# Turning six of eight token tiles with VectorE block transposes and SBUF transfers instead of TensorE transposes

## The chip, the cores and the metric

The kernel runs on one core of one Trainium2 chip. The metric is the device time of one execution in microseconds (us), lower is better. The core has five engines that run their own instruction streams and wait for each other through semaphores: TensorE (PE, matmuls), VectorE (DVE), ScalarE (ACT), GpSimd (POOL) and SyncE (SP), which here issues nearly all DMA transfers on one queue.

## The reference, cut to what matters

One layer of a hybrid decoder over 1024 tokens of width 1024, all in float32. Two branches (a Conformer convolution and a sliding-window attention) are merged into `mixed`; then

```python
h = layer_norm(DEEPNORM_ALPHA * h + mixed @ w_out, ln1_g, ln1_b)
up = causal_dwconv(h @ ffn_w_up, ffn_dw, ffn_dw_b)
u, g = jnp.split(up, 2, axis=-1)
f = (jax.nn.gelu(g, approximate=False) * u) @ ffn_w_down
return layer_norm(DEEPNORM_ALPHA * h + f, ln2_g, ln2_b)
```

The change concerns the step between the first `layer_norm` and `h @ ffn_w_up`. The layer norm works on rows of tokens (a token per partition, 1024 channels along the free dimension); the product with `ffn_w_up` needs `h` with channels on the partitions. Between the two, every tile of 128 tokens must be turned from 128 tokens x 1024 channels into 8 blocks of 128 channels x 128 tokens.

## The kernel before

Every float32 product is made of three matmuls of rounded parts: an operand is split into a high part (cast by ACT) and a low part (subtraction on DVE, or on POOL). The FFN products follow a Strassen-like scheme, in which sums of quadrants of `h` (called B11, B21, BT1 to BT4 and B22) are formed by DVE, split, and multiplied with sums of quadrants of the weights.

**The w_out stage.** The loop at line 1477 goes over the token tiles in the order 3, 7, 2, (the two leftover meta rows, -1), 6, 0, 4, 1, 5. `out_rows(i)` loads the tile's residual rows from DRAM (`h0d`) into one of two row buffers in `OB` (`RT`), multiplies in two halves of 512 channels (24 matmuls each, into PSUM tiles `ps_w` of which there are three), adds each half to the rows on DVE (L1339), collects the statistics (L1340, L261, ACT's L268 and three short DVE steps), normalises in place (L1361) and stores the rows to `h1d`. A row buffer is loaded anew when its rows have been stored and turned.

**The turn.** `turn(i, ...)` lets PE transpose the eight 128x128 blocks (L1375) into `ps_h`, and ACT evacuates each with the norm's gain and bias as per-partition scalars (L1385) into `h1F`, the place of the turned tile in `FA`. A tile is turned while the next tile is multiplied: its eight transposes stand between the two halves of the next tile (for tile 3 after the second half of tile 7), put there with `behind`. Tile 5, the last, is turned inside the first products of the FFN.

**The order of DVE.** For tiles 0, 4, 1 and 5 the DVE instructions are chained with `line(ins)`: each must come after the one before in program order, whether or not a later one would be ready. Chained are the adds, statistics and norms of these tiles (`pin = line`), and the work on the FFN's operands that lies between them: `w_first` (splits of up-projection weights, L1406 and sums L1423), `split_of(sub, q)` (cast on ACT at L1276, subtraction on DVE at L1281), and `form_t2`, `form_t3`, `form_t4` (sums of quadrants, L1285). `sub` 1 is the part of the tokens in tiles 2, 3, 6, 7, `sub` 0 that in tiles 0, 1, 4, 5, of which `EARLY` columns belong to tiles 0 and 4 and `LATE` ones to 1 and 5. What stands between a tile's halves is written in this table:

```python
work = {0: [(w_first, 2), (split_of, 1, B11), (split_of, 1, B21), (split_of, 1, B22)],
        4: [(w_first, 3), (split_of, 1, BT2), (w_first, 3), (form_t4, 1)],
        1: [(form_t3, 1), (split_of, 0, B11, EARLY), (form_t2, 0, EARLY), (w_first, 5)],
        5: [(w_first, 6)]}
```

`quadrant(sub, kk, h)` is half the channels (`kk`) of one pair of tiles: for `sub` 1, B11 and B21 come from tiles 2 and 3, B22 from tiles 6 and 7; for `sub` 0 and early columns, B11 comes from tile 0, and `form_t2` subtracts quadrants of tile 0 from those of tile 4 (first half of the channels, then second). After tile 4 come the splits of BT4 and BT1 of `sub` 1 and `edges` (two boundary columns, L1469).

DMA instructions are issued by SP (`load`) in the order that the scheduler gives them; only DVE's chain and PE's turns are ordered by hand here.

Of the kernel before, what the change touches and what calls it, by code (L numbers as in the profile page):

```python
# [25 lines left out]
AF = mybir.ActivationFunctionType  # L26
# [3 lines left out]
P = 128  # L30
D = 1024
KC = D // P
# [29 lines left out]
SUB = [(0, 258), (258, HW)]  # L62


RK_TURN, RK_SPLIT, RK_EVAC, RK_START, RK_QKV, RK_RESID, RK_ATT = 450, 500, 600, 1000, 10000, 20000, 30000
# [59 lines left out]
def tile_hybrid_layer(  # L125
# [3 lines left out]
    nc = tc.nc  # L129
# [5 lines left out]
    def load(o, i):  # L135
        return nc.sync.dma_start(out=o, in_=i)
# [5 lines left out]
    def f32(ap):  # L142
        return ap.bitcast(F)

    def after(ins, first):

        tc.add_manual_dep(ins.ins, first.ins.name, mybir.DependencyInfo(
            mybir.DependencyClass.NoSync, mybir.DependencyReason.SCHED_ONLY), reason="order of work")

    @contextmanager  # L150
    def rank(p):

        saved = tc.cur_priority
        tc.cur_priority = p
        yield
        tc.cur_priority = saved
# [10 lines left out]
    RHC = arena.tile([P, 8384], R, name="RHC")  # L167
    RHO = arena.tile([P, 8384], R, name="RHO")
    OB = arena.tile([P, 4 * U], F, name="OB")
# [6 lines left out]
    h0d = dpool.tile([U, D], F, name="h0d")  # L176
    h1d = dpool.tile([S, D], F, name="h1d")
# [39 lines left out]
    cols = const.tile([P, N_COLS], F, name="cols")  # L217
# [13 lines left out]
    g1col = lambda k: colA[:, 58 + k:59 + k]  # L231
    b1col = lambda k: colA[:, 66 + k:67 + k]
# [450 lines left out]
    bias, bias0 = (bias_t[:, a:b].rearrange("p (u h c) -> p u h c", u=2, h=NH // 2)  # L683
                   for a, b in ((0, NH * KW), (NH * KW, N_BIAS)))
# [60 lines left out]
    src = ps[:16, :P].rearrange("p (g d) -> p g d", d=HD)  # L745
    nc.scalar.copy(VA[:16, 0, :, 0], src)
    nc.vector.tensor_tensor(VA[:16, 0, :, 1], src, f32(VA[:16, 0, :, 0]), OP.subtract)
    for q4 in range(2):
# [4 lines left out]
        src = ps[:, :].rearrange("p (n g d) -> p n g d", g=2, d=HD)  # L753
# [31 lines left out]
    ahead = chunks_done[first_chunk + 2 * KC + 7]  # L785
# [6 lines left out]
    for h in range(NH):  # L792
        g, r = divmod(h, 4)
        o = ps[:2, h * 16:(h + 1) * 16]
# [34 lines left out]
    for g in range(NKV):  # L829
# [3 lines left out]
        src = ps[:16].rearrange("p (r q) -> p r q", r=4)[:, :, 0:2]  # L833
# [3 lines left out]
    for g in range(NKV):  # L837
        o = po[:, g * 8:g * 8 + 8]
# [21 lines left out]
    for i in range(NB):  # L860
        for g in range(NKV):
            q = load_q(g, i) if i else q0[g]
# [6 lines left out]
            for u in range(2):  # L869
# [3 lines left out]
                for h in range(2):  # L873
                    o = ps[:, h * KW:h * KW + w]
# [8 lines left out]
                if not i:  # L883
                    f = first[u]
                    src = ps[:, :2 * KW].rearrange("p (h c) -> p h c", h=2)
# [9 lines left out]
            for h in range(2):  # L895
                for u in range(2):
                    j = h * 2 + u
# [68 lines left out]
    OC = late.tile([P, 8320], R, name="OC")  # L966
# [124 lines left out]
    RT = OB[:, 0:2048]  # L1091
# [131 lines left out]
    def h1F(sub, h, k):  # L1223
        o = h1_at(sub, h * KC + k)
        return FA[:, o:h1_at(sub, h * KC + k + 1)]
# [28 lines left out]
    def line(ins):  # L1254

        if lined:
            after(ins, lined[-1])
        lined.append(ins)
        return ins
# [46 lines left out]
    def split_of(sub, q, cs=slice(None)):  # L1306
        b11, b12, b21, b22 = blocks(sub)
        src = {B11: b11, B21: b21, BT2: T2_AT[:, :b22.shape[1]], BT4: b21, BT1: b11, BT3: b12, B22: b22}[q]
        bsplit(sub, q, src, cs)
# [1 line left out]

    WO_ORDER = (4, 5, 0, 1, 2, 3, 6, 7)
    edge = const.tile([P, KC, 2], F, name="edge")
    r_next = [1]

    def out_rows(i, between=(), work=()):


        n, u = (P, 2 + i * P) if i >= 0 else (2, 0)
        if n == P:  # L1320
            o = r_next[0] % 2 * 1024
            r_next[0] += 1
            whole = RT[:, o:o + 1024]
            load(whole, h0d[u:u + n, :])
        else:
            whole = OB[:, 3072:4096]
        r = whole[:n]
        order = WO_ORDER if i != 5 else (0, 1, 2, 3, 6, 7, 4, 5)
        turned = None
        st = small.tile([P, 2, 6], F, name="st")  # L1330
        pin = line if i in (0, 4, 1, 5) else lambda ins: ins
        for half in range(2):
            hs = slice(half * 512, half * 512 + 512)
            ps = pat.tile([P, 512], F, name="ps_w", tag="mm", bufs=3)
            if n == P:
                last = product(ps, [(mixed(i, k, 0), mixed(i, k, 1), wo[k][0][:, hs], wo[k][1][:, hs])
                                    for k in order], turned)
                with rank(RK_TURN):
                    pin(nc.vector.tensor_tensor(r[:, hs], ps, r[:, hs], OP.add))  # L1339
                    pin(nc.vector.bn_stats(st[:, half], r[:, hs]))  # L1340
                turned = None
                if between[half:] and between[half]:
                    turned = turn(*between[half], behind=[last])
                if half == 0:
                    for f, *x in work:
                        f(*x)
                continue

            for j in range(4):
                nc.tensor.matmul(ps[:2], sel[:, j // 2 * 2:j // 2 * 2 + 2], two_parts[j // 2][j % 2][:, hs],  # L1350
                                 start=j == 0, stop=j == 3)
            nc.scalar.copy(r[:, hs], ps[:2])
        if n < P:
            q = FA[:2, 0:1024]
            load(q, h0d[0:2, :])
            nc.vector.tensor_tensor(r, r, q, OP.add)
        with rank(RK_TURN):
            (mu, rs), = ln_stats([(r, n)], half_stats=st if n == P else None)
            for a in (512, 0) if i == 5 else (None,):
                x = r if a is None else r[:, a:a + 512]  # L1360
                ins = pin(nc.vector.tensor_scalar(x, x, mu, rs, OP.subtract, OP.mult))  # L1361
        if n == P:
            load(h1d[u - 2:u - 2 + P, :], r)
        else:
            load(ed, r)
            for t in range(2):
                load(edge[:, :, t], dram(ed, t * D, [[1, P], [P, KC]]))
        return whole, n, ins

    def turn(i, r, n, ins, banks=None, behind=None, upper=False):  # L1370
        with rank(RK_TURN):
            for j, k0 in enumerate((4, 0) if upper else (0, 4)):
                ps = banks[j] if banks else pat.tile([P, 512], F, name="ps_h", tag="s", bufs=2)
                for k in range(4):
                    ins = nc.tensor.transpose(ps[:, k * P:(k + 1) * P], r[:, (k0 + k) * P:(k0 + k + 1) * P], ident)  # L1375
                    if behind:
                        after(ins, behind[-1])
                        behind.append(ins)
                for k in range(k0, k0 + 4):
                    src = ps[:, (k - k0) * P:(k - k0 + 1) * P]  # L1380
                    h, jj = divmod(i, 4)
                    sub = 0 if jj < 2 else 1
                    a = 2 + jj * P - SUB[sub][0]
                    dst = h1F(sub, h, k)[:, a:a + P]
                    nc.scalar.activation(dst, src, AF.Identity, bias=b1col(k), scale=g1col(k))  # L1385
        return behind[-1] if behind else None


    RING = [RHO[:, i * 1024:(i + 1) * 1024] for i in range(4)]
    RING += [None] * 4  # L1390
# [73 lines left out]
    def edges():  # L1464
        with rank(RK_TURN):
            first, second = (FA[:, h * 2064:h * 2064 + 2064].rearrange("p (k n) -> p k n", n=258)[:, :, 0:2]
                             for h in range(2))
            for t, c, op in ((edge, 58, OP.mult), (first, 66, OP.add)):
                line(nc.vector.tensor_tensor(first, t, colA[:, c:c + KC].unsqueeze(2).to_broadcast([P, KC, 2]), op))  # L1469
            nc.vector.memset(second, 0.0)  # L1470

    ahead = []
# [4 lines left out]
    for i in (3, 7, 2, -1, 6, 0, 4, 1, 5):  # L1477
        if i == -1:
            out_rows(i)
            continue  # L1480
        rows = out_rows(i, ahead, work.get(i, ()))
        ahead = [None, (i, *rows)] if i == 3 else [(i, *rows)]
        if i == 3:
            two_rows(7, rows[2])
        if i == 7:
            for a, (hi, lo) in zip(two_sum, two_parts):
                after(split(a, hi, lo, True), rows[2])
            two_stack.close()
            W2.append(wo_stack.enter_context(tc.tile_pool(name="w2", bufs=1, side="right", reuse_waits="tile")).tile(
                [P, 2048], R, name="W2"))  # L1490
        if i == 0:
            form_t2(1)
        if i == 4:
            split_of(1, BT4)
            split_of(1, BT1)
            edges()
        if i == 1:
            split_of(1, BT3)
            split_of(0, B21, EARLY)
            form_t3(0, EARLY)  # L1500
            form_t4(0, EARLY)
# [64 lines left out]
    for c in range(FC):  # L1566
# [8 lines left out]
        for subs in passes:  # L1575
            last = subs == passes[-1]
            w_next = iter(range(7))
            a, b = SUB[subs[0]][0], SUB[subs[-1]][1]
            i = max(a, 2)
# [189 lines left out]
    rows, stats = {}, {}  # L1769
# [159 lines left out]
```

## Time and profile before

| what | value |
|---|---|
| median of 3 runs | 1234.69 us (1234.56 to 1234.72) |
| profiled execution | 1234.65 us, span 1232.9 us, granted clock 0.998 |
| PE, DVE, ACT busy, share of the span | 99%, 88%, 47% |
| w_out stage on PE | 489.58 us (first `ps_w` matmul) to 587.66 us (first FFN matmul) |
| `ps_h` transposes in the stage | 56, 272 ns each by themselves, pipelined |
| DMA in the whole kernel | 210.62 MB, mean 171 GB/s |

All times are positions in one profiled execution, counted from the start of its span. In a row of a timeline the first number is the start, the second the duration (both us), then come the engine, the line of the kernel, the operation, output<-input and, in square brackets, how long the engine had been idle before and what it was waiting for. In the chain of waits a row gives start, duration, engine, output and line. PE's matmuls overlap, so the chain's durations (which add up) are used for PE.

### The profile page before, as it was taken

The page shows a single profiled execution, that of the slowest core. Times are in us where ns is not written, and L with a number is a line of the kernel's source. Part 1 is how long each engine was busy: PE and PEld are TensorE (multiplying, and loading weights), DVE is VectorE, ACT ScalarE, POOL GpSimd, SP SyncE. Part 2 cuts the span into 40 slices and gives each one's busy share as a digit, 9 for nine tenths or more (in the row PEclk, how much of TensorE's full clock was granted, in tenths as well). Part 3 has the DMA queues.
Part 4 walks back from the last instruction along what each step waited for, and adds up shares of the span by engine and source line. Part 5 has one row for each costly group of instructions (what it writes and reads, how often), then busy time and mean ns, then how long its engine had stood idle before and what let it go on. Part 6 is the DMA issues. An engine that isn't in the chain of part 4 may idle for free.

```text
span 1232.9 us, 21777 instructions
## 1 busy us (share of the span) xinstructions
PE 1223.6 (99%) x8564; PEld 1141.3 (93%) x8564; DVE 1084.5 (88%) x1840; ACT 584.4 (47%) x1065; POOL 15.0 (1%) x19
## 2 busy tenths in 40 slices
PE   9999999999999999999999999999999999999997
PEld 8999999999999999888999999999999998888886
DVE  8899989999879798659899999998999986995697
ACT  7532346654265233435655545555455553544331
POOL 1000000000000010000000000000000000000000
PEclk9999999999999999999999999999999999999999
DMA  7284834412255544322255555554465568997722
GB/s 280 74 277 101 213 96 112 129 55 73 85 153 175 180 140 136 116 73 87 69 182 197 193 191 197 191 187 137 167 210 190 182 230 305 395 334 295 255 87 86
DMA packets 104726, 210.62 MB, mean 171 GB/s; under 512 B 28520, under 2 KB 42394, under 8 KB 104624
## 3 DMA queue, kind: packets, MB, share of 16 engines
q1 hardware_dynamic: 88624, 198.16, 48.6%
q10 hardware_dynamic: 16000, 11.07, 2.9%
q8 instruction: 67, 1.10, 0.4%
q14 instruction: 35, 0.29, 0.1%
HBM read 147.59 MB, written 60.38 MB: 169 GB/s over the span
## 4 chain that ended last, share of the span: by engine, by line
PE 98%; DVE 1%; ACT 0%; issue 0%; DMA 0%; POOL 0%; DVEq 0%; POOLq 0%
PE px L1596 14%; PE py L1596 9%; PE ps_x L1742 9%; PE ps_z L330 8%; PE ps_z L329 8%; PE ps_z L325 8%; PE ps_z L1742 8%; PE pw L1596 5%; PE pz L1596 5%; PE ps_p L325 2%; PE ps_p L329 2%; PE ps_p L330 2%; PE ps_w L329 2%; PE ps_w L330 2%; PE ps_w L325 2%; PE ps_z L565 2%
## 5 line engine op out<-in xcount | busy, mean ns | idle before, releaser
L715 DVE SCALAR_TENSOR_TENSOR FA<-cin,cols,FA 128x1026 f32<-128x1026 f32 x120 | 152.3, 1278 | 0.9
L330 PE MATMUL ps_z<-RHO,wlo 128*128 128x256 f32 (+2 forms) x324 | 103.6, 320 | 0.0
L329 PE MATMUL ps_z<-RHO,whi 128*128 128x256 f32 (+2 forms) x324 | 103.5, 319 | 0.0
L330 PE MATMUL ps_z<-RHC,wlo 128*128 128x256 f32 (+2 forms) x324 | 103.4, 319 | 0.0
L329 PE MATMUL ps_z<-RHC,whi 128*128 128x256 f32 (+2 forms) x324 | 103.4, 319 | 0.0
L325 PE MATMUL ps_z<-RHC,whi 128*128 128x256 f32 (+2 forms) x324 | 103.2, 319 | 0.0
L325 PE MATMUL ps_z<-RHO,whi 128*128 128x256 f32 (+2 forms) x324 | 103.2, 318 | 0.0
L294 ACT CAST whi<-wr 128x1024 fp32r<-128x1024 f32 x37 | 38.9, 1051 | 107.4 <-PE ps_z L329 85.1
L1405 ACT CAST RHO<-wr 128x512 fp32r<-128x512 f32 x92 | 55.3, 619 | 26.2 <-DMA wr<-in_w_up_dram 12.2
L1406 DVE TENSOR_TENSOR RHO<-wr,RHO 128x512 fp32r<-128x512 f32 x92 | 62.4, 690 | 5.2 <-ACT RHO L1405 4.9
L325 PEld LDWEIGHTS ps_z<-RHO,whi 128*128 128x128 f32 x324 | 60.9, 188 | 4.5
L329 PEld LDWEIGHTS ps_z<-RHO,whi 128*128 128x128 f32 x324 | 60.9, 188 | 4.2
L325 PEld LDWEIGHTS ps_z<-RHC,whi 128*128 128x128 f32 x324 | 60.9, 188 | 4.1
L329 PEld LDWEIGHTS ps_z<-RHC,whi 128*128 128x128 f32 x324 | 61.0, 188 | 4.1
L330 PEld LDWEIGHTS ps_z<-RHO,wlo 128*128 128x128 f32 x324 | 61.0, 188 | 4.0
L330 PEld LDWEIGHTS ps_z<-RHC,wlo 128*128 128x128 f32 x324 | 61.0, 188 | 3.9
L1423 DVE TENSOR_TENSOR wr<-wr 128x512 f32<-128x512 f32 x88 | 60.9, 692 | 0.2
L297 DVE TENSOR_TENSOR wlo<-wr,whi 128x1024 fp32r<-128x1024 f32 x35 | 42.7, 1221 | 12.0 <-ACT whi L294 11.6
L1608 ACT COPY FA<-px 128x514 f32<-128x514 f32 (+2 forms) x23 | 13.1, 569 | 71.1 <-PE px L1596 71.0
L1405 ACT CAST ws<-wr 128x512 fp32r<-128x512 f32 x60 | 36.1, 618 | 20.9 <-DVE wr L1423 11.8
L722 ACT ACTIVATE FA<-ps_z,cols 128x258 f32<-128x258 f32 (+2 forms) x48 | 26.1, 543 | 39.4 <-PE ps_z L330 39.0
L1406 DVE TENSOR_TENSOR ws<-wr,ws 128x512 fp32r<-128x512 f32 x60 | 40.6, 688 | 3.6 <-ACT ws L1405 3.5
(487 smaller groups left out, 3492.2 us busy)
## 6 DMA issues: line engine op xcount, KB each, us to landing
wr<-in_w_up_dram SPq DMA_DIRECT2D x44, 512.0 KB
wr<-in_w_z_dram SPq DMA_DIRECT2D x30, 512.0 KB
fd<-FA SPq DMA_DIRECT2D x44, 256.0 KB
OB<-in_w_down_dram SPq DMA_DIRECT2D x19, 512.0 KB
qt<-qd SPq DMA_DIRECT2D x28, 256.0 KB
td<-OB SPq DMA_DIRECT2D x12, 512.0 KB
sums<-fd SPq DMA_DIRECT2D x12, 512.0 KB
sd<-sums SPq DMA_DIRECT2D x12, 512.0 KB
```

Source lines behind the costliest of these rows:

```text
L294: ins = nc.scalar.copy(hi, raw)
L297: return (nc.vector if quick else nc.gpsimd).tensor_tensor(lo, raw, f32(hi), OP.subtract)
L325: ins = nc.tensor.matmul(ps, ah, bh, start=i == 0, stop=False)
L329: nc.tensor.matmul(ps, ah, bl, start=False, stop=False)
L330: last = nc.tensor.matmul(ps, al, bh, start=False, stop=i == n - 1)
L715: nc.vector.scalar_tensor_tensor(acc[c], cin[:, j:j + U], wc, acc[c], OP.mult, OP.add)
L722: nc.scalar.activation(t, ps, AF.Tanh, bias=bcol(14 + i), scale=0.5)
L1405: nc.scalar.copy(hi, src)
L1406: ins = nc.vector.tensor_tensor(lo, src, f32(hi), OP.subtract)
L1423: ins = nc.vector.tensor_tensor(*x)
L1596: ins = nc.tensor.matmul(o, x[:, ks], bmat(sub, q, hl, k), start=first and k + j == 0, stop=k == 3 and j == 2, skip_group_check=not first)
L1742: nc.tensor.matmul(bank[:, cs], l[:, ts], r[:, ws], start=first and a and x + k == 0, stop=z and x == len(ops) - 1 and k == 2, skip_group_ ...
```

## The change

Six tiles (3, 7, 2, 6, 0, 4) are no longer turned by PE. For each of them `turn_dma` lets DVE transpose the 32x32 blocks of the normalised rows (one instruction of 128x1024) into a buffer in `OB` (one place for tiles 3, 7, 2, 6, another for 0, 4), and then moves the blocks between partition groups with 16 transfers from SBUF to SBUF, each of 32 partitions by 256 words, into a place in `OC` or `RHC`. ACT's eight evacuations per tile read that place instead of PSUM. Tiles 1 and 5 are turned by PE as before.

The stores of the rows, the transfers and the row loads of all tiles are chained in a written order (`in_turn`): store of tile i, its 16 transfers, the row load of the tile after next, and so on. In DVE's written order the transposes of tiles 0 and 4 are entries of their own (`line`): tile 0's behind its norm, tile 4's behind the splits of BT4 and BT1 and ahead of `edges`. Those of tiles 3, 7, 2 and 6 come after their norm and are not in the chain. The table `work` is unchanged.

```diff
+    NROW = (3, 7, 2, 6, 0, 4, 1, 5)
+    NEXT_ROWS = dict(zip(NROW, NROW[2:]))
+    moves, fetched = [], {}
+
+    def in_turn(ins):
+        if moves:
+            after(ins, moves[-1])
+        moves.append(ins)
+
+    def fetch(i):
+        o = (NROW.index(i) + 1) % 2 * 1024
+        fetched[i] = RT[:, o:o + 1024]
+        in_turn(load(fetched[i], h0d[2 + i * P:2 + (i + 1) * P, :]))
...
-            o = r_next[0] % 2 * 1024
-            r_next[0] += 1
-            whole = RT[:, o:o + 1024]
-            load(whole, h0d[u:u + n, :])
+            if i not in fetched:
+                fetch(i)
+            if not moves[1:]:
+                fetch(NROW[1])
+            whole = fetched[i]
...
                 if between[half:] and between[half]:
                     turned = turn(*between[half], behind=[last])
+                    if between[half][0] in NEXT_ROWS:
+                        fetch(NEXT_ROWS[between[half][0]])
...
-            load(h1d[u - 2:u - 2 + P, :], r)
+            in_turn(load(h1d[u - 2:u - 2 + P, :], r))
...
+    TURN_AT = {3: (OC, 4144, 2048), 7: (OC, 5168, 2048), 2: (OC, 6192, 2048), 6: (OC, 7216, 2048), 0: (RHC, 2096, 3072), 4: (RHC, 3120, 3072)}
+
+    def turn_dma(i, r, norm):
+        t, o, b = TURN_AT[i]
+        blocks, cols = OB[:, b:b + 1024], f32(t[:, o:o + 1024])
+        with rank(RK_TURN):
+            ins = nc.vector.transpose(blocks.rearrange("p (q k j) -> p q k j", q=4, k=KC),
+                                      r.rearrange("p (k q j) -> p q k j", k=KC, q=4))
+            after(ins, norm)
+            if i in (0, 4):
+                line(ins)
+            for a in range(4):
+                for q in range(4):
+                    in_turn(load(cols[32 * q:32 * q + 32, a * 256:(a + 1) * 256],
+                                 blocks[32 * a:32 * a + 32, q * 256:(q + 1) * 256]))
+            if i in NEXT_ROWS:
+                fetch(NEXT_ROWS[i])
...
+            src = cols.rearrange("p (a k j) -> p k a j", a=4, k=KC)
+            for k in range(KC):
+                nc.scalar.activation(h1F(sub, h, k)[:, a:a + P].rearrange("p (a j) -> p a j", a=4), src[:, k],
+                                     AF.Identity, bias=b1col(k), scale=g1col(k))
...
         rows = out_rows(i, ahead, work.get(i, ()))
-        ahead = [None, (i, *rows)] if i == 3 else [(i, *rows)]
+        ahead = [] if i in TURN_AT else [(i, *rows)]
+        if i in TURN_AT and i != 4:
+            turn_dma(i, rows[0], rows[2])
...
         if i == 4:
             split_of(1, BT4)
             split_of(1, BT1)
+            turn_dma(i, rows[0], rows[2])
             edges()
```

More of the change, by code (lines that the diff above doesn't have):

```diff
@@ L1313, in tile_hybrid_layer @@
     edge = const.tile([P, KC, 2], F, name="edge")
-    r_next = [1]
+    NROW = (3, 7, 2, 6, 0, 4, 1, 5)
[9 more added lines that the diff above has]
+        in_turn(load(fetched[i], h0d[2 + i * P:2 + (i + 1) * P, :]))
     def out_rows(i, between=(), work=()):
@@ L1386, in turn @@
         return behind[-1] if behind else None
+    TURN_AT = {3: (OC, 4144, 2048), 7: (OC, 5168, 2048), 2: (OC, 6192, 2048), 6: (OC, 7216, 2048), 0: (RHC, 2096, 3072), 4: (RHC, 3120, 3072)}
[14 more added lines that the diff above has]
+                fetch(NEXT_ROWS[i])
+            h, jj = divmod(i, 4)
+            sub = 0 if jj < 2 else 1
+            a = 2 + jj * P - SUB[sub][0]
+            src = cols.rearrange("p (a k j) -> p k a j", a=4, k=KC)
+            for k in range(KC):
+                nc.scalar.activation(h1F(sub, h, k)[:, a:a + P].rearrange("p (a j) -> p a j", a=4), src[:, k],
+                                     AF.Identity, bias=b1col(k), scale=g1col(k))
     RING = [RHO[:, i * 1024:(i + 1) * 1024] for i in range(4)]
```

## The prediction

> **What bounds the kernel now.** I read the page first, then the chain of work that ended last around the changed stage, then each engine's timeline between 488 and 606 us, and last the DMA issues of SP.
>
> ```profile
> PE 1223.6 (99%) x8564; PEld 1141.3 (93%) x8564; DVE 1084.5 (88%) x1840; ACT 584.4 (47%) x1065; POOL 15.0 (1%) x19
> ```
>
> TensorE (PE) is busy for 99% of the span, so whatever is taken off it is worth time, as long as nothing else becomes late. The chain, from the turn of tile 1 on:
>
> ```profile
> 581.50 0.87 PE ps_h L1375 x8
> ...
> 587.83 1.41 PE px L1596 x12
> ...
> 602.65 1.15 DVE OA L1281
> 603.85 1.58 PE pw L1596 x11
> ```
>
> Eight PE transposes of one tile cost 0.87 us of the chain. The w_out stage ends at 587.83, where the first product of the FFN starts. At 603.85 the chain passes from VectorE (DVE) to PE: there DVE is already level with PE. How full DVE is inside the stage (columns: PE, PEld, DVE, ACT, POOL busy, clock, DMA share, GB/s):
>
> ```profile
> 544.20:585.70 41.50, 41.50 (x201) 34.71 (x200) 36.87 (x59) 21.57 (x48) 0.00 (x0) 1.00 0.24 90
> ```
>
> DVE works 36.87 of 41.50 us, in an order written out by hand, so it stands still whenever the head of that order is not ready. These are the entries on which the change acts:
>
> ```profile
> 540.73 0.69 DVE L1339 TENSOR_TENSOR OB<-ps_w,OB 128x512 f32<-128x512 f32 x1 [4.91 <-PE ps_w L330]
> ...
> 543.34 0.81 DVE L1361 TENSOR_SCALAR OB<-OB,mv,sd 128x1024 f32<-128x1024 f32 x1
> ...
> 546.18 0.69 DVE L1339 TENSOR_TENSOR OB<-ps_w,OB 128x512 f32<-128x512 f32 x1 [2.03 <-PE ps_w L330]
> ...
> 550.98 1.22 DVE L1281 TENSOR_TENSOR RHC<-FA,RHC 128x1024 fp32r<-128x1024 f32 x1
> 552.53 0.69 DVE L1339 TENSOR_TENSOR OB<-ps_w,OB 128x512 f32<-128x512 f32 x1 [0.32 <-PE ps_w L330]
> ...
> 571.18 0.17 DVE L1469 TENSOR_TENSOR FA<-edge,cols 128x16 f32<-128x16 f32 x1
> ...
> 574.87 0.70 DVE L1285 TENSOR_TENSOR FA<-FA 128x520 f32<-128x520 f32 x1
> 575.60 0.70 DVE L1285 TENSOR_TENSOR OB<-FA 128x520 f32<-128x520 f32 x1
> ...
> 579.43 0.81 DVE L1361 TENSOR_SCALAR OB<-OB,mv,sd 128x1024 f32<-128x1024 f32 x1
> ...
> 587.87 0.69 DVE L1339 TENSOR_TENSOR OB<-ps_w,OB 128x512 f32<-128x512 f32 x1 [2.14 <-PE ps_w L330]
> ```
>
> In order: tile 6's second half is added, after 4.91 us of waiting for PE; its norm ends (543.34+0.81 = 544.15); tile 0's first half is added; the split of B22 (sub 1), which needs tiles 6 and 7; tile 0's second half; the edges, right behind the splits after tile 4's norm; the two subtractions of form_t2 (sub 0, early columns), which need tile 4; tile 1's norm, end 580.24; the last half of tile 5.
>
> **The change, part by part.**
>
> *Removed.* 6 tiles x 0.87 us = 5.2 us of PE. Three of the six (tiles 3, 7, 2) lie ahead of tile 0, so tile 0 begins 2.6 us earlier.
>
> *Added on DVE.* Per tile one block transpose of 128x1024 f32; the trace has none. Bounds: 0.81 (L1361) and 2.44, twice the 1.22 of L1281; both rows have the same shape. I take 1.2, the duration of L1281, nearest in shape (it too rewrites 128x1024 words into another buffer; L1361 works in place). Nothing below zero is possible for an added instruction. Tile 6's falls into the 2.03 us in which DVE waited at 546.18 and is hidden there, though its consumers see it; those of tiles 0 and 4 stand in the written order and cost 1.2 each.
>
> *Added on SP.* Per tile 16 transfers of 32 partitions by 1 KB, all on SP's one queue behind the tile's store, and the next row load behind them. The SP rows:
>
> ```profile
> 534.53 0.24 SPq L136 DMA_DIRECT2D ed<-OB  x1
> ...
> 569.02 0.32 SPq L136 DMA_DIRECT2D h1d<-OB  x1
> 571.69 0.32 SPq L136 DMA_DIRECT2D OB<-h0d  x1
> ...
> 1160.90 0.47 SPq L136 DMA_DIRECT2D FA<-fd  x1
> 1161.41 0.47 SPq L136 DMA_DIRECT2D OB<-in_w_down_dram  x1
> ```
>
> The pitch of back-to-back issues is bounded by 0.29 us (0.24 of the smallest, plus the 0.05 by which 0.47 misses the start of the next) and 0.51 (two loads of 512 KB). I take 0.38, nearer the small end, because a transfer has 32 rows. Landing (SP's waits: what it waited for, us in total, times, longest):
>
> ```profile
> SPq L136 <- DMA h1d<-OB: 12.7, 5, 3.1
> ```
>
> The load at 571.69 waited for the store of 569.02, so 512 KB land within 2.67 us of issue. Without the time of the bytes (512 KB at some 390 GB/s, a rate in the rows further down, is 1.3) about 1.4 would be left. I take 1.8. From the transpose's end to the last landing that is 0.1 + 15 x 0.38 + 1.8 = 7.6 us (5.9 to 10.4). The Trainium skill ("DMA: Bandwidth & Descriptors", section "Anatomy of one DMA — SWDGE (gpsimd) path") puts a fixed 2.0 us on a DMA, most of it the write's receipt; as an estimate from it 7.9 instead of 7.6, and 0.6 more in the result below. Its "VectorE: DVE Perf Modes" (section "Rules for kernel authors") speaks against the whole change: a 128x128 transpose belongs on TensorE where a PSUM destination will do, which it did here.
>
> *On ACT* the eight evacuations remain and now read SBUF; I keep their time, and the cast of B22 behind them:
>
> ```profile
> 546.62 2.90 ACT L1385 ACTIVATE FA<-ps_h,cols 128x128 f32<-128x128 f32 x8 [3.90 <-PE ps_h L1375]
> 549.55 1.05 ACT L1276 CAST RHC<-FA 128x1024 fp32r<-128x1024 f32 x1
> ```
>
> *First new wait, B22 behind tile 6.* Norm end 544.15 - 2.6 = 541.55; transpose to 542.75; transfers to 550.35; evacuation to 553.25; cast to 554.3. DVE gets there at 550.98 - 2.6 = 548.4, so it stands for 5.9 us, with tile 0's second half and everything later queued behind. Against before, B22's split is late by 3.3 and the next entry by 3.0 (the 0.32 at 552.53 goes). PE doesn't feel it yet: its three PSUM buffers let it run on.
>
> *Second new wait, form_t2 behind tile 4.* With tile 0's transpose, DVE is 4.2 late; tile 4's transpose runs from 571.18 + 4.2 = 575.4 to 576.6. form_t2 is reached at 574.87 + 5.4 = 580.3, but its first half needs four evacuations of tile 4 (half of 2.90): 576.6 + 7.6 + 1.45 = 585.65. Its second half needs all eight: 587.1, against 575.60 before. DVE is now 11.5 late.
>
> *What this does to PE.* Tile 1 is still turned by PE, between the halves of tile 5, and its norm stands behind form_t2 on DVE: norm end 580.24 + 11.5 = 591.7. PE, 5.2 early, arrives at 576.3 and stands for 15.4 us. The turn begins 10.2 later than before (591.7 against 581.50), and so does the FFN. DVE would be at tile 5's last half at 585.73 + 11.5 = 597.2 (587.87 less its 2.14 of waiting), before PE's 598.0, so PE ends last, and the rest follows as before.
>
> *The clock after the stop.* No row shows PE after a long stop inside the kernel; the nearest are its first microseconds (the warm-up matmuls alone: PE, PEld, clock, DMA share, GB/s):
>
> ```profile
> 3.00:4.00 1.00, 1.00 (x6) 1.00 (x6) 1.00 0.97 369
> 4.00:5.00 1.00, 1.00 (x7) 1.00 (x6) 1.00 1.05 414
> ...
> 6.00:7.00 1.00, 1.00 (x11) 1.00 (x11) 1.00 1.05 275
> 7.00:8.00 1.00, 1.00 (x11) 1.00 (x11) 1.00 0.95 389
> ```
>
> From a standstill 6 to 7 a microsecond, from 6 us on 11: some 5 us at 0.6 of the rate, 1.8 us lost. Between 0 and 1.8 I take 1.8, because the stop of 15 us is of the kind that the start has. By the Trainium skill ("TensorE: Matmul & The Clock Gate", section "Part 1: The HAM clock gate (the "warmup" mystery)") a window of about 3.4 us without work halves the clock until another window is busy: an estimate of 1.7 us for one stop, and none for stops under 3 us.
>
> *Edits at no cost.* The other tiles' transposes and transfers (3, 7, 2) lie where DVE waits for PE (4.91 us at 540.73); their first consumers are the splits of B11 and B21, the two entries ahead of B22's, so at about 546, after tile 2's 7.6 us have run out. Without that cover they'd lengthen the first wait. The row loads now stand behind 16 issues; each is issued a tile ahead.
>
> *Sum.* -5.2 of PE, + 15.4 of standing, + 1.8 of clock = +12.0 us. The profiled execution took 1234.65 us (span 1232.9 and 1.75 around it), the median of the three is 1234.69, so the same within 0.04: 1246.7 us.
>
> **The rivals.**
>
> *The transfers land in time: faster.* If the pipe of transfers takes under 1.7 us, neither wait opens (the first closes at 548.4 - 542.75 - 3.95 = 1.7). DVE still has two more transposes in its order, so tile 1's norm ends at 580.24 - 2.6 - 0.3 + 2.4 = 579.7 and the turn comes 1.7 earlier than before: 1232.9. With the transpose at 0.81 it would be 2.5 earlier, and 5.2, 1229.4, is the floor. Against it: sixteen issues alone take 3.7 us at the smallest duration quoted. For it: a queue may take equal small issues faster than any row shows.
>
> *Both waits, but short.* Pitch 0.29 and landing 1.4 make 5.9; two waits in a row save 2 x 1.7 = 3.4, and a full clock 1.8: +6.8, 1241.5; with the short transpose three times (tiles 6, 0, 4) 1240.3.
>
> *The queue is the bound.* Pitch 0.51 and landing 2.67 make 10.4: 2 x 2.8 = 5.6 more, 1252.3. A transpose of 2.44 adds 3.7 more.
>
> *The clock doesn't fall.* As forecast without the 1.8: 1244.9.
>
> **How the numbers follow.** Two waits of about the size worked out, with either clock: 0.60 (1242.5 to 1250). Short waits 0.13, queue-bound 0.14. Transfers in time and faster by over 0.2% (2.5 us, about what a measurement of this kernel can tell from no change) 0.07, within 0.2% 0.06. So faster 0.07, same 0.06, slower 0.87; time 1246.7. The range from 1239 to 1254 takes in the short waits and most of the queue-bound case.
>
> **What would show it.** Right: on DVE, idle time of 4 to 8 us ahead of the split of B22 and ahead of form_t2, both ending with ACT's evacuations, and these ending with DMA; on PE one stop of over 10 us ahead of tile 1's turn, followed by matmuls at a longer pitch; on SP issues at 0.3 to 0.5 us; L1375 with 16 instead of 64 transposes. Wrong: no idle time at those two entries, or a PE without a stop, or a pipe of transfers shorter than 2 us; a transpose of over 2 us would shift the loss from the transfers to DVE.

## The result, and the profile after

The changed kernel takes 1269.25 us (median, 1268.18 to 1270.22), the kernel before 1234.64: ratio 1.028, 95% interval 1.0264 to 1.0296. It is slower, as forecast, but by 34.6 us, not 12.0, and outside the range. The profiled execution took 1268.18 us (span 1266.4), 33.5 more than that of before.

The page after, the counterpart of the first line shown of before (busy time and share of the span by engine), and PE's waits (what waited for what: us in total, times, longest):

```profile
PE 1224.3 (97%) x8516; PEld 1139.5 (90%) x8516; DVE 1090.5 (86%) x1846; ACT 586.6 (46%) x1065; POOL 15.0 (1%) x19
```

```profile
PE ps_h L1390 <- DVE OB L1376: 20.9, 1, 20.9
PE ps_w L325 <- DVE OB L1352: 11.0, 3, 7.7
```

PE has 48 transposes fewer and isn't less busy: it stood still four times, and ran slowly after three of these stops. The longest stop is ahead of tile 1's turn, where it was expected; three more, ahead of matmuls whose PSUM buffer waits for DVE's add, were not. Whose lateness it is stands in DVE's timeline (lines have moved: L1410 is the new block transpose, L1352 the add, L1376 the norm, L1426 ACT's evacuation of a turned tile; L1281, L1285, L1276 and L268 are as before):

```profile
526.49 1.25 DVE L1410 STREAM_TRANSPOSE OB<-OB 128x1024 f32<-128x1024 f32 x1 [6.25 <-DMA OC<-OB]
...
539.59 1.25 DVE L1410 STREAM_TRANSPOSE OB<-OB 128x1024 f32<-128x1024 f32 x1 [2.79 <-DMA OC<-OB]
...
552.25 1.25 DVE L1410 STREAM_TRANSPOSE OB<-OB 128x1024 f32<-128x1024 f32 x1 [5.16 <-DMA OC<-OB]
...
554.65 0.69 DVE L1352 TENSOR_TENSOR OB<-ps_w,OB 128x512 f32<-128x512 f32 x1 [1.15 <-DMA OB<-h0d]
...
570.46 1.22 DVE L1281 TENSOR_TENSOR RHC<-FA,RHC 128x1024 fp32r<-128x1024 f32 x1 [10.93 <-ACT RHC L1276]
...
588.99 0.16 DVE L276 SCALAR_TENSOR_TENSOR sd<-mv,sd 128x1 f32<-128x1 f32 x1 [1.71 <-ACT sd L268]
...
592.58 1.24 DVE L1410 STREAM_TRANSPOSE OB<-OB 128x1024 f32<-128x1024 f32 x1
...
606.86 0.70 DVE L1285 TENSOR_TENSOR FA<-FA 128x520 f32<-128x520 f32 x1 [9.71 <-ACT FA L1426]
...
608.39 0.70 DVE L1285 TENSOR_TENSOR OB<-FA 128x520 f32<-128x520 f32 x1 [0.84 <-ACT FA L1426]
```

The two waits of the forecast are there: 10.93 us ahead of B22's split (570.46, against 550.98 before) and 9.71 + 0.84 ahead of form_t2 (second half 608.39, against 575.60). New are the three waits of a block transpose for transfers (14.2 in all): each of tiles 7, 2 and 6 waits until the 16 transfers of the tile ahead have left the block buffer that four tiles share. New too are the adds that wait for a row load. SP's timeline says why (issues of a kind grouped, their number at the end):

```profile
540.87 10.02 SPq L136 DMA_DIRECT2D OC<-OB  x16
550.93 0.59 SPq L136 DMA_DIRECT2D OB<-h0d  x1
551.56 1.05 SPq L136 DMA_DIRECT2D edge<-ed  x2
552.71 1.69 SPq L136 DMA_DIRECT2D h1d<-OB  x1
554.49 10.08 SPq L136 DMA_DIRECT2D OC<-OB  x16
564.61 0.58 SPq L136 DMA_DIRECT2D OB<-h0d  x1
```

Sixteen transfers occupy SP for 10.02 to 10.08 us, 0.63 each, where 0.38 was taken and 0.51 was the upper end. The chain from there to the FFN:

```profile
603.27 1.88 DMA RHC<-OB
...
605.18 3.19 ACT FA L1426 x8
...
608.39 0.70 DVE OB L1285
...
613.08 1.97 PE ps_h L1390 x8
615.05 0.43 PE ps_w L325
...
616.74 0.23 PE ps_w L329
...
621.32 1.41 PE px L1639 x12
```

The last transfer lands 1.88 us after its issue begins. PE turns tile 1 at 613.08 instead of 581.50 (+31.6); the eight transposes take 1.97 instead of 0.87 and the first matmuls come at 0.43 instead of 0.23. From the turn to the FFN it is 8.24 us, against 6.33: +1.9. So the FFN starts at 621.32 instead of 587.83, 33.5 later, which is the whole difference; behind it the two kernels run alike.

### The profile page after: what moved, and what is told of

It is laid out like the page before. It is cut to its first block, busy times and chain, and to the rows that moved or that the text cites. A ratio compares the mean times of both kernels' runs of the same rounds, so it can differ in the third digit from the quotient of the medians.

```text
span 1266.4 us, 21860 instructions
## 1 busy us (share of the span) xinstructions
PE 1224.3 (97%) x8516; PEld 1139.5 (90%) x8516; DVE 1090.5 (86%) x1846; ACT 586.6 (46%) x1065; POOL 15.0 (1%) x19
## 4 chain that ended last, share of the span: by engine, by line
PE 90%; SPq 4%; DVE 3%; DMA 1%; ACT 1%; issue 1%; POOL 0%; DVEq 0%; ACTq 0%; POOLq 0%
PE px L1639 14%; PE py L1639 9%; PE ps_x L1785 9%; PE ps_z L330 8%; PE ps_z L329 8%; PE ps_z L325 8%; PE ps_z L1785 7%; PE pw L1639 5%; PE pz L1639 5%; SPq L136 4%; PE ps_p L325 2%; PE ps_p L329 2%; PE ps_p L330 2%; PE ps_z L565 2%; PE ps_o L925 1%; PE ps_s L876 1%
## 5 line engine op out<-in xcount | busy, mean ns | idle before, releaser
L1445 ACT CAST RHO<-wr 128x512 fp32r<-128x512 f32 x92 | 55.5, 618 | 28.4 <-DVE wr L1463 13.1
L1651 ACT COPY FA<-px 128x514 f32<-128x514 f32 (+2 forms) x23 | 13.1, 571 | 75.1 <-PE px L1639 75.1
L1639 PE MATMUL px<-OA,RHO 128*128 128x258 f32 (+1 forms) x336 | 43.9, 279 | 0.0
```

The lines of the kernel that those rows point to most:

```text
L1445: nc.scalar.copy(hi, src)
L1639: ins = nc.tensor.matmul(o, x[:, ks], bmat(sub, q, hl, k), start=first and k + j == 0, stop=k == 3 and j == 2, skip_group_check=not first)
```

## The experiments

In the expectations, theory A says: the two places of the forecast are right, and their size comes from the pace at which SP issues these transfers, together with what that pace makes of the written order. Differences are against the kernel before unless said otherwise.

**Which tiles cost what.** The first kernel turns only tiles 3, 7, 2 and 6 in the new way, the second only 0 and 4.

```diff
-    TURN_AT = {3: ..., 7: ..., 2: ..., 6: ..., 0: ..., 4: ...}
+    TURN_AT = {3: ..., 7: ..., 2: ..., 6: ...}     # second kernel: {0: ..., 4: ...}
```

> Tiles 3, 7, 2 and 6 are turned by VectorE and transfers, tiles 0 and 4 by TensorE again. Theory A (the pitch of 0.63 us at which SP issues sixteen transfers per tile makes two waits in DVE's written order, one at B22 behind tile 6 and one at form_t2 behind tile 4): the first wait stays whole, B22 late by some 19 us as with all six, the second is gone. 18 us over the kernel before, 1251 to 1255 us. Rival B (the added block transposes in DVE's full stretch after 546 us are the cost): those of tiles 0 and 4 are gone, so no slower than 1237 us.

> Only tiles 0 and 4 are turned by VectorE and transfers. Theory A: no wait at B22; at form_t2 DVE waits for tile 4 as with all six (some 10 us), the second subtraction comes 12 to 13 us later than before, TensorE stops ahead of tile 1's turn and runs on a slow clock after it: 1246 to 1250 us. Rival B (block transposes on DVE): 2.4 us more at most, 1237 us. Rival C (the one block buffer that tiles 3, 7, 2, 6 share is what paces the stage): nothing of it is left here, under 1238 us.

Measured 1254.21 us (ratio 1.0158, 1.0143 to 1.0173) and 1250.68 (1.0128, 1.0111 to 1.0145), the second 0.7 above theory A's bounds. DVE's timeline of the first kernel, then of the second:

```profile
570.50 1.23 DVE L1281 TENSOR_TENSOR RHC<-FA,RHC 128x1024 fp32r<-128x1024 f32 x1 [10.88 <-ACT RHC L1276]
```

```profile
588.51 0.70 DVE L1285 TENSOR_TENSOR FA<-FA 128x520 f32<-128x520 f32 x1 [9.71 <-ACT FA L1426]
...
590.05 0.70 DVE L1285 TENSOR_TENSOR OB<-FA 128x520 f32<-128x520 f32 x1 [0.84 <-ACT FA L1426]
```

The first four tiles bring the wait at B22 with the same 10.9 us, and no wait at form_t2; the other two bring just the latter, as long as with six. 19.5 and 16.0 make 35.5, against 34.6 with all six: the two parts add. The second kernel has only two transposes, none of which waits for its block buffer, and still loses 16.0, so neither DVE's own work nor the shared buffer can be the whole.

**The price of an issue.** The kernel before, with groups of 12 transfers each appended at its end.

```diff
+    for x in range(12):       # SBUF to SBUF, 32 partitions x 1 KB
+        one(a[q:q + 32, x * 256:(x + 1) * 256], OB[s:s + 32, x * 256:(x + 1) * 256])
+    ...                       # 128 partitions; from h0d with 32 and 128; to h1d; SBUF to SBUF, 32 x 128 B
```

> The kernel before, with six groups of twelve transfers issued back to back by SP after its last store: SBUF to SBUF 32 partitions x 1 KB, SBUF to SBUF 128 x 1 KB, DRAM to SBUF 32 x 1 KB, DRAM to SBUF 128 x 1 KB, SBUF to DRAM 32 x 1 KB, SBUF to SBUF 32 x 128 B. The time of the whole is of no interest, the pitch of each group is. If 32 partitions make an issue slow: 0.6 us in groups 1, 3, 5 and 6 and 0.4 in groups 2 and 4. If a source in SBUF makes it slow: 0.6 in groups 1, 2, 5, 6 and 0.4 in 3 and 4. If the bytes make it slow: 0.6 in group 1, more in group 2, under 0.4 in group 6.

```profile
1226.30 3.68 SPq L136 DMA_DIRECT2D RHO<-OB  x6
...
1231.17 9.65 SPq L136 DMA_DIRECT2D RHO<-OB  x15
1240.89 11.37 SPq L136 DMA_DIRECT2D RHC<-h0d  x24
1252.30 5.61 SPq L136 DMA_DIRECT2D h1d<-OB  x12
1257.94 7.53 SPq L136 DMA_DIRECT2D OC<-OB  x12
```

The last three rows: 11.37 / 24 = 0.47 us for loads from DRAM (32 and 128 partitions alike), 5.61 / 12 = 0.47 for stores to DRAM, 7.53 / 12 = 0.63 for transfers within SBUF, these of 128 bytes a partition. Those of 1 KB came at about the same pace: 3.68 / 6 = 0.61 on 32 partitions, and 9.65 / 15 = 0.64 in a group of which twelve are on 128. So among these groups an issue is dear where both ends are in SBUF; neither the number of partitions nor the bytes matter. That is none of the cases as they were expected. It is a price for issues back to back: after a pause a single row load takes 0.32 to 0.33 us (0.32 at 571.69 before), while the one right behind 16 transfers took 0.58 to 0.59 (550.93, 564.61 above).

**The shared block buffer.** Tiles 7 and 6 get a block buffer of their own, which lies over part of the turned tiles, so that these values change.

```diff
-    7: (OC, 5168, 2048), ... 6: (OC, 7216, 2048)
+    7: (OC, 5168, None), ... 6: (OC, 7216, None)
-        blocks, cols = OB[:, b:b + 1024], ...
+        blocks, cols = FA[:, 4112:5136] if b is None else OB[:, b:b + 1024], ...
```

> All six tiles as in the change, but tiles 7 and 6 use a second block buffer, so that a block transpose doesn't wait until the tile before has been moved. Theory A: SP's queue with 10 us of issues, a store and a row load per tile is then the pace of the first four tiles (11.2 us instead of 13.1); DVE's waits ahead of the block transposes (14.2 us in all) nearly go, B22 comes some 6 us earlier, the rest stays: 1262 to 1265 us. Rival C (the shared buffer is the main loss): the first wait goes, 1250 us or less.

1265.79 us (1.0251, 1.0236 to 1.0267). DVE's waits:

```profile
DVE OB L1352 <- DMA OB<-h0d: 17.6, 3, 8.0
```

The transposes no longer wait; the adds do, for row loads that stand behind 16 issues: 17.6 us where it was 4.5. The buffer was one of two ways into the same queue; closing it gives back 3.5 us, 0.8 short of theory A's bounds, and B22 comes 2.8 us earlier (567.70), not 6.

**The written order.** Row loads ahead of the transfers, and a second block buffer in a free place.

```diff
+            if i in NEXT_ROWS:
+                fetch(NEXT_ROWS[i])
             for a in range(4):
...
-            if i in NEXT_ROWS:
-                fetch(NEXT_ROWS[i])
```

> All six tiles with sixteen transfers each, but the row load stands ahead of a tile's transfers and tiles 7 and 6 have a block buffer of their own. Theory A: the waits of DVE for row loads and for the block buffer go, but SP still needs 11 us per tile: B22 at about 564 instead of 570, the second wait as before: 1260 to 1264 us. Rival E (the place of the row loads behind the transfers is what the stage loses): the first wait shrinks to that of the forecast, 1252 us or less.

1270.74 us (1.0291, 1.0277 to 1.0305): nothing gained, against theory A's number as well as the rival's. SP's timeline:

```profile
539.60 0.53 SPq L136 DMA_DIRECT2D h1d<-OB  x1
...
542.48 0.35 SPq L136 DMA_DIRECT2D OB<-h0d  x1
542.88 10.01 SPq L136 DMA_DIRECT2D OC<-OB  x16
...
554.24 0.52 SPq L136 DMA_DIRECT2D h1d<-OB  x1
557.50 0.33 SPq L136 DMA_DIRECT2D OB<-h0d  x1
```

The row load overwrites the rows that the store ahead of it takes away, so it waits for that store to land (539.60 to 542.48, 554.24 to 557.50), and now 16 transfers stand behind that wait. Theory A's number had reckoned the load as ready to go. In either order a tile holds SP, waits included, longer (here 14.6 us, 539.60 to 554.24) than it holds PE (10.9 us before, reckoned below).

**A second queue.** Half of the transfers issued by GpSimd, or by ACT.

```diff
+                    if q % 2:
+                        nc.gpsimd.dma_start(out=o, in_=x)      # second kernel: nc.scalar
+                    else:
                         in_turn(load(o, x))
```

> All six tiles as in the change, but eight of a tile's sixteen transfers (the odd q) are issued by GpSimd, which is idle in the stage, and eight by SP. Theory A (each issue occupies its queue for 0.63 us, and that sets the pace): if GpSimd issues at 0.9 us or faster, a tile needs 5 to 7 us of issuing, no block transpose waits for the buffer, and both waits shrink to about what the forecast supposed: 1246 to 1253 us. Rival D (what the transfers share behind the queues sets the pace): no gain, 1266 us or more.

> The same with ACT issuing the odd half. Theory A: the pace of SP halves as well, but ACT does its work in order, so eight issues and the wait for the block transpose stand ahead of casts and square roots that DVE needs: 1248 to 1260 us. Rival D: 1266 us or more.

GpSimd: 1312.92 us (1.0637, 1.0622 to 1.0651). ACT: 1255.82 (1.0172, 1.0158 to 1.0185), 13.4 less than with SP alone. GpSimd's timeline:

```profile
528.04 0.51 POOL L1419 DMA_DIRECT2D OC<-OB  x1 [1.51 <-issue]
530.01 0.51 POOL L1419 DMA_DIRECT2D OC<-OB  x1 [1.46 <-issue]
```

GpSimd issues one in 2.0 us, so eight take longer than SP's sixteen, and the condition of theory A (0.9 us or faster) isn't met: this run decides nothing between A and D. With ACT each queue has eight and the loss shrinks by 13.4 of 34.6 us: the same data, moved in the same pieces, at twice the pace of issues, so D is out. SP's and ACT's issues for tile 4 run side by side, each at 0.6 to 0.7 us an issue:

```profile
585.42 4.98 SPq L136 DMA_DIRECT2D RHC<-OB  x8
```

```profile
585.42 5.31 ACTq L1419 DMA_DIRECT2D RHC<-OB  x8
```

**The same data by five transfers.** All six tiles, each with four stores to DRAM and one load.

```diff
             for a in range(4):
-                for q in range(4):
-                    in_turn(load(cols[32 * q:32 * q + 32, ...], blocks[32 * a:32 * a + 32, ...]))
+                in_turn(load(dram(bd[i], a * 256, [[D, 32], [32 * D, 4], [1, 256]]),
+                             blocks[32 * a:32 * a + 32].rearrange("p (q x) -> p q x", q=4)))
+            in_turn(load(cols, bd[i][:, :]))
```

> All six tiles and the written orders as in the change, but the blocks go to DRAM with four stores and come back with one load: five issues of 0.47 us and 0.33 us in place of sixteen of 0.63 us, with one more landing of some 2.5 us. Theory A (the number of issues at their pitch is the loss): from the block transpose to the landing 7 us instead of 11.4, which is near the length that the forecast supposed, so its own sum applies: 9 to 13 us over the kernel before, 1243 to 1248 us. Rival D (landing and bytes, not issues): no gain, 1265 us or more.

1260.13 us (1.0205, 1.0191 to 1.0219), well above what theory A expected and below rival D's 1265, though tile 4's pipe was as short (587.57 + 1.24 to the evacuation's start at 597.02, 8.2 us). The loss has another place now. DVE's and ACT's timelines (lines shifted by one: L269 is the square root, L1427 the evacuation):

```profile
547.98 0.16 DVE L277 SCALAR_TENSOR_TENSOR sd<-mv,sd 128x1 f32<-128x1 f32 x1 [7.55 <-ACT sd L269]
```

```profile
544.57 3.19 ACT L1427 ACTIVATE FA<-OC,cols 128x128 f32<-128x128 f32 x8 [9.51 <-DMA OC<-bd]
547.67 0.28 ACT L269 ACTIVATE sd<-mv,eps 128x1 f32<-128x1 f32 x1
```

Tile 6's norm waits 7.55 us for a square root of 0.28, because that stands on ACT's queue behind tile 2's evacuations, which wait for a transfer (9.51 us). To test this, the evacuations of a tile are queued behind the next tile's square root:

```diff
+                ins = nc.scalar.activation(h1F(sub, h, k)...)
+                if k == 0 and i not in (6, 4):        # second kernel: if i not in (6, 4):
+                    after(ins, rstds[-1])
```

> The way through DRAM for all six tiles (five issues per tile), with the evacuations of a tile queued on ACT behind the next tile's reciprocal square root (not for tiles 6 and 4). The run without that order lost 7.2 us where the square root of tile 6 stood on ACT behind evacuations that waited for DRAM, and 4 us where a weight cast did. Theory A with ACT's order as the second part: those 11 us go: 1247 to 1251 us. If ACT's order costs nothing: 1258 us or more.

> All six tiles, 4 stores and 1 load through DRAM, as before, but all eight evacuations of tiles 3, 7, 2 and 0 are queued on ACT behind the reciprocal square root of the tile that follows. Theory A (ACT's in-order queue is what keeps the short pipe from showing): the 7 us that tile 6's norm waits for ACT go, B22's split waits less than 4 us instead of 7.5, and the time falls to 1247 to 1251. Rival F (the wait comes from elsewhere, tile 6's own pipe or the row loads): 1257 or more, with the square root of tile 6 early and the norm or B22 late all the same. In between, a part of it.

The first of the two held back one evacuation of eight only; the scheduler put the other seven ahead of it, so they stood before the square root as ever. Its 1259.17 us (1.0199, 1.0183 to 1.0214) say nothing on the theory. The second holds all eight: 1251.24 us (1.0135, 1.0121 to 1.0149), 8.9 less. Its ACT and DVE timelines (L271 the square root, L1434 the evacuation, L1284 and L1288 the split and form_t2):

```profile
540.37 0.30 ACT L271 ACTIVATE sd<-mv,eps 128x1 f32<-128x1 f32 x1 [5.53 <-DVE mv L264]
544.62 3.19 ACT L1434 ACTIVATE FA<-OC,cols 128x128 f32<-128x128 f32 x8 [3.95 <-DMA OC<-bd]
```

```profile
558.01 1.23 DVE L1284 TENSOR_TENSOR RHC<-FA,RHC 128x1024 fp32r<-128x1024 f32 x1 [6.87 <-ACT RHC L1279]
...
591.07 0.70 DVE L1288 TENSOR_TENSOR OB<-FA 128x520 f32<-128x520 f32 x1 [0.84 <-ACT FA L1434]
```

The square root comes 7.3 us earlier (540.37 instead of 547.67), B22 4.7 earlier (562.67 before the edit) and form_t2 9.2 earlier (600.24), about the 8.9 of the time. Most of what form_t2 gains beyond B22 is a cast of weights, behind tile 0's evacuations on ACT, for which DVE had waited 4.0 us. So theory A has the cause of the gain, with the time 0.2 above its bounds, but B22 still waits 6.87, more than the 4 expected. That part is rival F's, tile 6's own pipe, as SP's timeline shows:

```profile
541.10 1.06 SPq L136 DMA_DIRECT2D edge<-ed  x2
542.21 3.48 SPq L136 DMA_DIRECT2D h1d<-OB  x1
545.73 2.49 SPq L136 DMA_DIRECT2D bd<-OB  x4
```

The issue of tile 6's row store, right behind the two edge loads, holds SP for 3.48 us where such a store takes 0.32 elsewhere (562.60), and tile 6's blocks stand behind it. Why it takes so long was not tested.

**Fewer tiles.** Only tiles that lie far ahead of their consumers: 3 and 7 by 16 transfers (row loads first, two buffers); 3 and 7 through DRAM, the row load between the stores and the load; 3, 7 and 2 so, with the evacuations held back as above; and 3, 7, 2 and 6 through DRAM, with B22's split moved behind tile 4's first half.

```diff
-    TURN_AT = {3: ..., 7: ..., 2: ..., 6: ..., 0: ..., 4: ...}
+    TURN_AT = {3: ..., 7: ...}
...
+            if i in NEXT_ROWS:
+                fetch(NEXT_ROWS[i])
+            in_turn(load(cols, bd[i][:, :]))
```

> Only tiles 3 and 7 are turned by VectorE and sixteen transfers, with the row loads ahead of the transfers and two block buffers; their first consumers come at 549 us. Theory A: no wait opens, TensorE saves twice 0.87 us: 1232.5 to 1233.5 us. Rival B (a block transpose on DVE costs what it takes): no gain or a loss of up to 2.4 us, 1234.7 to 1237 us.

> Only tiles 3 and 7, by four stores and one load through DRAM, with the row load between the stores and the load. With sixteen transfers in SBUF the same two tiles came out level (1234.48 against 1234.68 us), after a row load that came 3.5 us late. Theory A: nothing waits here, TensorE saves 1.7 us, of which the FFN may lose some 0.7 as it did there: 1233.0 to 1234.0 us. If the block transposes cost what they take: 1235 us or more.

> Tiles 3, 7 and 2 through DRAM, their evacuations queued on ACT behind the reciprocal square root of the tile that follows. Theory A: a third tile off PE is worth up to 0.87 us more than the two of the run with tiles 3 and 7 (1233.15), if its evacuations no longer stand before tile 6's square root: 1232.0 to 1233.2. Rival G (tile 2's evacuations, now queued behind that square root, come too late for the splits of B11 and B21, or the row loads do): 1234 to 1238.

> Tiles 3, 7, 2 and 6 by VectorE and the way through DRAM (four stores, row load, one load), with the split of B22 moved behind tile 4's first half in DVE's written order. Theory A: the pipe of some 7 us ends ahead of every consumer, TensorE saves four times 0.87 us: 1231 to 1233 us. If the pipe is 2 us longer the splits of B11 and B21 wait for tile 2 and the gain is gone: 1234 to 1238 us.

| tiles | us | ratio (95%) | idle time on DVE that it brings |
|---|---|---|---|
| 3, 7, within SBUF | 1234.48 | 0.9999 (0.9990 to 1.0008) | 3.52 for a row load |
| 3, 7, through DRAM | 1233.15 | 0.9987 (0.9979 to 0.9996) | none over 0.4 |
| 3, 7, 2, through DRAM | 1235.68 | 1.0008 (0.9999 to 1.0017) | B11 1.56, B22 2.82 |
| 3, 7, 2, 6, through DRAM | 1243.56 | 1.0073 (1.0060 to 1.0085) | tile 6's norm 7.35, for ACT's square root |

The first of them misses theory A's bounds by 1.0 us and is level with the kernel before, as rival B had it; yet its profiled execution (1234.23 us) is 1.2 us ahead at tile 5's last half (586.68 for 587.87 on DVE) and still 1.0 ahead at the issue of the last output (1228.06 for 1229.07), so nothing to speak of is lost in the FFN. The span ends 0.5 ahead (1232.4 for 1232.9); why the median over all executions isn't ahead is open. Two tiles through DRAM are the one version that beats the kernel before clear of noise, by 1.55 us of the 1.74 that two turns take of PE, within theory A's bounds. In the chain of its profiled execution, the rows of the turn and of the FFN's start:

```profile
580.27 0.87 PE ps_h L1391 x8
...
586.61 1.41 PE px L1639 x12
```

Both come 1.2 us earlier than before (581.50 and 587.83). With tile 2 as the third, its evacuations come too late for the splits of B11 and B21: the rival of that run holds. Four tiles miss both numbers of their run: tile 6's norm waits 7.35 us for a square root behind tile 2's evacuations, which are not held back here, as with all six.

## Why the prediction was wrong in size

**Right.** The direction; both places of waiting and what ends them (evacuations, which end with DMA); the stop of PE ahead of tile 1's turn; the transpose (1.24 to 1.25 us for 1.2); the landing (1.88 for 1.8); the clock (1.9 for 1.8 at that stop). On the clock, the window of the after trace around the last stop, and behind it (busy time of PE, PEld, DVE, ACT and POOL, then the granted clock, the DMA share and GB/s):

```profile
596.00:616.00 20.00, 2.92 (x11) 2.73 (x12) 8.92 (x17) 6.29 (x16) 0.00 (x0) 0.50 0.24 76
616.00:618.00 2.00, 2.00 (x9) 1.55 (x9) 1.97 (x4) 2.00 (x6) 0.00 (x0) 0.85 0.00 0
618.00:620.00 2.00, 2.00 (x10) 1.66 (x9) 0.51 (x1) 0.79 (x2) 0.00 (x0) 1.00 0.49 143
```

Half the clock in the stop, and the full clock some 3.7 us after the restart (613.08 to 616.74). The rule of the Trainium skill that the prediction named ("TensorE: Matmul & The Clock Gate", section "Part 1: The HAM clock gate (the "warmup" mystery)": a window of about 3.4 us, half the clock) agrees with that. The fixed 2.0 us per DMA that the Trainium skill states ("DMA: Bandwidth & Descriptors", section "Anatomy of one DMA — SWDGE (gpsimd) path") agrees with the landing of 1.88, on a queue other than the one it was stated for. That 1.8 us met 1.9 is in part luck: it was 5 us at 0.6 of the rate, read from rows whose granted clock is 1.00, and here it was 3.7 us at half. The estimate of no loss for stops under 3 us doesn't hold in this trace: after the stop of 2.08 us that ends at 530.09, ahead of which PE had only the eight small matmuls of the two meta rows, the granted clock was 0.50 between 532 and 534.

**The term that was mis-sized: the issue.** 0.38 us was taken, between 0.29 and 0.51; 0.63 was measured. The bounds came from transfers with an end in DRAM, and the nearest rows were passed over. The tile va of the trace of before has transfers within SBUF (groups: min/median/max in ns):

```profile
L136 SPq DMA_DIRECT2D va<-va x2: 617/932/1247, 80.5 to 81.8; - x2
L136 SPq DMA_DIRECT2D va<-v x2: 642/667/692, 85.9 to 86.6; - x2
```

None is under 0.617. Taken from them, 16 issues would have been 10 us and the forecast's own sum 7.5 us larger (two pipes, 15 x 0.25 each), before the next step. The small end itself was a single issue after a pause (0.24); back to back, issues with one end in DRAM came at 0.47. The reason given for it, fewer rows per transfer, is refuted by the issue groups: 32 and 128 partitions cost the same. "DMA: Bandwidth & Descriptors" of the Trainium skill has a rule that would have warned (section "Rules for kernel authors"): under 64 KB a transfer is mostly overhead and many should be made one. Here 32 KB in 0.63 us are 52 GB/s, and five transfers in place of 16, in a kernel otherwise the same, saved 9.1 us (1260.13 for 1269.25).

**The step that failed: "edits at no cost".** The prediction charged nothing for the rate at which tiles follow each other. At 0.38 a tile would have held the queue and the shared buffer for 1.25 + 0.1 + 16 x 0.38 + 1.88 = 9.3 us, less than the 10.9 that PE needs for a tile (540.73 to 552.53 between second halves before, less the turn of 0.87). At 0.63 it is 13.3, and each tile waits for the one ahead: the block transposes of the after trace start 13.1 and 12.7 us apart (526.49, 539.59, 552.25). The price of an issue was worked into the pipe of one tile and not into the rate of tiles. The sentence on row loads ("each is issued a tile ahead") asked when they are issued, and not when the queue gets to them. And where PE was to run on with its three PSUM buffers, it stood three times for a late add of DVE, 11.0 us in all.

**The sum, step by step.** Tile 6's transpose starts at 552.25, not 541.55: +10.7, from the ring of queue and buffers in which each tile waits for the one ahead. SP is still at the store, so the transfers begin 0.9 later; from first issue to evacuation it is 11.68 (554.49 to 566.17) instead of 7.5: +4.2; evacuation and cast +0.4. So B22 is 16.2 later than forecast. From B22 to tile 4's transpose it is 22.12 instead of 21.08 (+1.0; 1.71 us of waiting at 588.99, for a square root queued on ACT behind an evacuation), and from there, 593.82, to form_t2's second half 14.57 instead of 10.5: +4.1. Together 21.3 of the 21.5 us that the forecast lacks (33.5 less 12.0). That ring and pipes hang on the issues is shown by two runs. With five transfers and ACT's order mended, tile 6's transpose starts at 542.13, and with two queues at 548.24; with two queues the pipes of tiles 6 and 4 are 7.3 and 7.5 us, from the transpose's end to the evacuation, where tile 4's was 11.4. How 10.7 divides between buffer and row loads is not shown, since each takes over when the other goes.

**What the forecast was right about, then.** With five transfers and ACT's order mended, the pipe of tile 4 is 7.8 us (580.03 to 587.85) where 7.6 was reckoned, and the loss is 16.6 us where 12.0 was: B22 at 558.01 for 554.3, form_t2's second half at 591.07 for 587.1. What is over comes ahead of B22, mostly in tile 6's pipe (10.3 us, 543.38 to 553.71), with its late row store. That 7.8 meets 7.6 is no support for 0.38, since the blocks went another way, with five issues and two landings.

**What the forecast left out: ACT's queue.** The evacuations were counted on ACT as if only their own consumers waited for them. On the way through DRAM the run with all eight held back shows 8.9 us for what was queued behind; in the changed kernel it is the 1.71 us at 588.99. The Trainium skill says it of ACT and DVE ("TensorE: Matmul & The Clock Gate", section "Architectural detail: the array is 16× 32×32, not 1× 128×128"): they take their instructions strictly in order. The traces agree: a square root of 0.28 us 7.3 us late.

**The rivals.** "The queue is the bound" named the right mechanism and stopped at 1252.3, because it capped the pitch at 0.51 and added it to the two pipes alone. Transfers in time, short waits and an unchanged clock didn't come.

## What to carry to other kernels

Price an issue from rows with the same two ends (SBUF to SBUF, DRAM to SBUF) that stand back to back, and compare issues times price per tile with the tile's time on the bound engine before reckoning any single delay: over that rate the cover is used up within a few tiles, as here. An evacuation on ACT that waited for a DMA held up what was queued behind it (here a square root of 0.28 us), so list such instructions as one lists the consumers of its result. Work is worth moving off a full engine where its consumers are far behind: two of six tiles gained 1.55 us, all six lost 34.6.

## What the runs showed of the hardware that was not expected

- On SP's queue, back to back, an issue took 0.63 us with both ends in SBUF, whatever the partitions (32 or 128) and the bytes (128 or 1024 a partition), and 0.47 with one end in DRAM, for loads on 32 and 128 partitions alike. After a pause a row load took 0.32 to 0.33, right behind 16 such transfers 0.58.
- GpSimd issued the same transfers at one in 2.0 us.
- Tile 4's way through DRAM (four stores, a wait for them, a load) took 7.8 and 8.2 us in two runs from the transpose's end to the evacuation, less than the 11.4 of 16 transfers within SBUF (593.82 to 605.18).
- A row store right behind two small edge loads held SP for 1.69 us (552.71) and, in the run with ACT's order mended, 3.48, where such a store took 0.32 elsewhere.
